# Differential attention on one core: the value products of a head written by block of keys instead of by block of queries

## The chip, the core and the metric

The kernel runs on one core of a Trainium2 chip. The core has TensorE (PE in the rows, with its weight loads as PEld), VectorE (DVE), ScalarE (ACT), GpSimd (POOL) and the queue that issues most transfers (SP). The metric is the device time of one execution in microseconds, lower is better, as the median of several runs.

## What is computed

The program is two transformer blocks over 512 tokens of width 1024. The change lies in the second block, in its differential attention with four heads; each head has two softmax maps over keys of 64 dimensions, and one value matrix of 128 columns:

```python
def diff_attention_causal(q, k, v, lam):
    ...
    def block(args):
        q_blk, i = args                                  # 128 queries
        s = jnp.einsum('bhmqd,bhmkd->bhmqk', q_blk, k).astype(jnp.float32) * scale
        s = jnp.where(kpos[None, :] <= qpos[:, None], s, -jnp.inf)
        p = jax.nn.softmax(s, axis=-1)
        a = p[:, :, 0] - lam * p[:, :, 1]
        return jnp.einsum('bhqk,bhkd->bhqd', a.astype(v.dtype), v)
...
        dq = rms_norm(dq, diff_q_gain[l])
        dk = rms_norm(dk, diff_k_gain[l])
        o_diff = diff_attention_causal(dq, dk, dv, lam)
        o_diff = rms_norm(o_diff, diff_subln[l]) * (1.0 - lam_init)
```

Beside it the block has a retention branch, whose products (rv, rq, rk, rg below) come next in the program, then the output product, cross attention and a feed-forward part.

## The kernel before

Every large product takes three passes of TensorE over split operands (a high and a low part of each, helper `mm3`, lines 199 to 201): `ws` makes one tile of 128 output columns for all 512 tokens with 8 x 3 products of 512 columns, `ts` one block of 128 tokens. Weights are loaded by SP into `wraw` (three buffers) and split by ACT (line 181) and DVE (line 182) into `whi` and `wlo`. The products write to a PSUM pool named `mm` with two banks; when a tile is complete, its evacuation function empties it. A second pool, `tp`, has two banks too, and a third, `at2`, has two pairs of banks.

The section of the change runs so: `ts` makes the values `dvn` of all four heads; then for heads 0 and 1, and after that for heads 2 and 3, `ws` makes the queries (two tiles, evacuated by `ev_dq`) and the keys (two tiles, `ev_dk`), and `diff_head(h)` is called for each of the two heads. The evacuation (`qk_norm`) copies the tile to `raw` on DVE, squares it on ACT, splits the squares (`sq`, `sqh`, `sql`), sums them on PE into a bank of `tp` (line 318), takes Ln and Exp on ACT (lines 310 and 311, tile `rb`), and multiplies on DVE (lines 1189 and 1196).

`diff_head(h)` takes a bank of `tp` for the transposed output `oT` of the head at its very beginning. For each of four blocks of 128 queries, i = 0 to 3, it makes the scores of both maps against the i + 1 blocks of keys that the mask leaves (line 1210, a pair of `at2`), subtracts the mask and finds the maxima on DVE, takes the exponentials on ACT (line 1217), combines the maps on DVE (lines 1219 and 1220), transposes each block of 128 x 128 on PE (line 1223), copies the transposed blocks to `aT` on ACT (line 1225), and multiplies each block of keys with the values into 128 columns of `oT` (line 1227). After the last block of queries `oT` is normed: squares and their split (`hsq`, `hsqh`, `hsql`), sums on PE into `at2`, Ln and Exp (`hrb`), the multiply on DVE (line 1231), which is the last that reads `oT`, and the split into `mxd`.

The order is not written by hand. A scheduler puts the instructions of each engine in a fixed order when the program is built; it pulls the products of the next stage (the queries and keys of heads 2 and 3 during heads 0 and 1, the retention values `rv` after that) into the gaps of the softmax. Each engine then works in that order, and waits at an instruction whose operands or buffers are not ready.

Of the kernel before, what the change touches and what calls it, by code (L numbers as in the profile page):

```python
# [8 lines left out]
F32 = mybir.dt.float32  # L9
# [11 lines left out]
S = 512  # L21
# [61 lines left out]
def body(tc, a, out):  # L83
    nc = tc.nc
    V, A, T, G = nc.vector, nc.scalar, nc.tensor, nc.gpsimd
    es = ExitStack()

    def pool(name, bufs, side=None, space=None, stack=None):
        kw = {}
        if side:  # L90
            kw["side"] = side
        if space is not None:
            kw["space"] = space
        return (stack or es).enter_context(tc.tile_pool(name=name, bufs=bufs, **kw))
# [21 lines left out]
    def psum(tag, name="ps"):  # L116
        if tag == "at":
            return banks[1][0].tile([128, 512], F32, name=name, tag="at", bufs=banks[1][1])
        return ps.tile([128, 512], F32, name=name, tag=tag, bufs=2)

    def psum2(tag="at2"):
        return banks[1][0].tile([128, 2, 512], F32, name=tag, tag=tag, bufs=banks[1][2])
# [141 lines left out]
    def hilo(hi, lo, src):  # L264
        A.copy(hi, src)  # L265
        last_lo[:] = [V.tensor_sub(lo, src, hi.bitcast(F32))]  # L266
# [40 lines left out]
    def rms_bcast(m, n, p, w=S, rbufs=2, name="rb"):  # L307

        q = p.tile([128, S], F32, name=name, bufs=rbufs)[:, :w]
        A.activation(q, m, AF.Ln, bias=epsc, scale=1.0 / n)  # L310
        A.activation(q, q, AF.Exp, scale=-0.5)
        return q
# [847 lines left out]
    tb = pool("tb", 1, side="right", stack=tst)  # L1160

    def tmp_(name, bufs):
        return tb.tile([128, S], F32, name=name, tag=name, bufs=bufs)
# [3 lines left out]
    def pair_(name, bufs):  # L1167
        return tb.tile([128, 2, S], F32, name=name, tag=name, bufs=bufs)

    w2 = a["w_in_2"][0]  # L1170
    dqn, dkn, dvn = {}, {}, {}

    def sq_sums(tag, ones, o, name):
        q = tmp_(name, 1)
        A.activation(q, o, AF.Square)
        hl = [tb.tile([128, S], F32R, name=name + n, bufs=2 if name == "sq" else 1) for n in "hl"]
        hilo(*hl, q)
        return sums(tag, ones, *hl)

    def qk_norm(o):  # L1180
        raw = tmp_("raw", 4)
        V.tensor_copy(raw, o)
        return raw, rms_bcast(sq_sums("tp", ones64r, o, "sq"), 64, tb)

    def ev_dq(c):
        def f(t, o):
            raw, rb = qk_norm(o)
            dqn[c + t] = slot2("dq")
            V.scalar_tensor_tensor(dqn[c + t], raw, gq8, rb, op0=OP.mult, op1=OP.mult)
        return f  # L1190

    def ev_dk(c):
        def f(t, o):
            raw, rb = qk_norm(o)
            dkn[c + t] = slot2("dk")
            V.scalar_tensor_tensor(dkn[c + t], raw, col("diff_k_gain_2"), rb, op0=OP.mult, op1=OP.mult)
        return f
# [4 lines left out]

    def diff_head(h):
        oT = psum("tp")
        for i in range(4):
            n = 128 * (i + 1)
            o = psum2()
            for m in range(2):
                ms = slice(64 * m, 64 * m + 64)
                T.matmul(o[:, m, :n], dqn[h][ms, i * 128:(i + 1) * 128], dkn[h][ms, :n], start=True, stop=True)  # L1210
            V.tensor_add(o[:, :, n - 128:n], o[:, :, n - 128:n], negdf[:, None, :].to_broadcast([128, 2, 128]))
            st = sp.tile([128, 2, 3], F32, name="dmx", bufs=4)
            V.reduce_max(st[:, :, 0], o[:, :, :n], axis=AX)
            V.tensor_scalar(st[:, :, 0], st[:, :, 0], -1.0, None, op0=OP.mult)
            pp = pair_("pp", 3)[:, :, :n]
            for m in range(2):
                A.activation(pp[:, m], o[:, m, :n], AF.Exp, bias=st[:, m, 0:1], accum_out=st[:, m, 1:2])
            V.reciprocal(st[:, :, 2], st[:, :, 1])
            V.tensor_scalar(pp[:, 1], pp[:, 1], st[:, 1, 2:3], lam, op0=OP.mult, op1=OP.mult)
            V.scalar_tensor_tensor(pp[:, 0], pp[:, 0], st[:, 0, 2:3], pp[:, 1], op0=OP.mult, op1=OP.subtract)  # L1220
            pt = o[:, 0, :n]
            for j in range(i + 1):
                T.transpose(pt[:, j * 128:(j + 1) * 128], pp[:, 0, j * 128:(j + 1) * 128], ident)  # L1223
            aT = tmp_("aT", 2)[:, :n]
            A.copy(aT, pt)
            for j in range(i + 1):
                T.matmul(oT[:, i * 128:(i + 1) * 128], dvn[j][:, h * 128:(h + 1) * 128], aT[:, j * 128:(j + 1) * 128],  # L1227
                         start=(j == 0), stop=(j == i))
        rb = rms_bcast(sq_sums("at2", onesr, oT, "hsq"), 128, tb, rbufs=1, name="hrb")
        y = tmp_("hsq", 1)  # L1230
        V.scalar_tensor_tensor(y, oT, gdf[:, h:h + 1], rb, op0=OP.mult, op1=OP.mult)
        for i in range(2):
            mx[i][4 + h] = mp.tile([128, S], F32R, name="mxd", tag="mxd", bufs=8)
        hilo(mx[0][4 + h], mx[1][4 + h], y)

    ts(w2, 8, 3072, 4, hT, ev_dv)
    for c in (0, 2):
        ws(w2, 8, 2048 + c * 128, 2, hT, S, ev_dq(c))
        ws(w2, 8, 2560 + c * 128, 2, hT, S, ev_dk(c))
        for h in (c, c + 1):  # L1240
            diff_head(h)
# [13 lines left out]
        A.copy(rg[t], o)  # L1255

    def rotated(o, scale):
        raw = tmp_("raw", 4)
        A.activation(raw, o, AF.Copy, scale=scale)
        sw = tmp_("sw", 2)  # L1260
        for g in range(4):
            src = g ^ 1
            nc.scalar.dma_start(sw[g * 32:(g + 1) * 32, :], raw[src * 32:(src + 1) * 32, :])
        V.tensor_mul(raw, raw, ct)
        V.tensor_mul(sw, sw, st_)
        return raw, sw

    def ev_rq(c):
        def f(t, o):
            raw, sw = rotated(o, 1.0)  # L1270
            rq[c + t] = slot2("rq")
            V.tensor_add(rq[c + t], raw, sw)
        return f

    def ev_rk(c):
        def f(t, o):
            raw, sw = rotated(o, 0.125)
            rk_[c + t] = slot2("rk")
            V.tensor_add(rk_[c + t], raw, sw)
        return f  # L1280
# [65 lines left out]
    oT = (xa.tile([128, 8, S], F32R, name="xoh"), xa.tile([128, 8, S], F32R, name="xol"))  # L1346
# [67 lines left out]
    aT = (fp.tile([128, NH, S], F32R, name="aTh"), fp.tile([128, NH, S], F32R, name="aTl"))  # L1414
# [58 lines left out]
```

## Time and profile before

| | |
|---|---|
| time, median of 3 runs | 1596.85 us (1596.2 to 1598.96) |
| time of the profiled execution | 1597.8 us |
| span of the profiled execution | 1596.0 us |
| PE busy | 1555.6 us, 97% of the span |
| DVE, ACT busy | 945.1 us (59%), 821.0 us (51%) |
| mean granted clock of PE | 0.996 |
| value products of the four heads (line 1227) | 80 records, first start 884.0 us, last 964.9 us |
| differential attention, first score to last value product | 876.4 to about 965 us |

Starts are counted from the beginning of the span. The page divides the span into 40 slices of about 40 us; the section of the change lies in the 22nd to 24th. A product of float32 operands is recorded as two records, so that the 40 value products stand as 80. A record of a product lasts beyond the start of the next one, since they are pipelined: what a product costs the engine is read from start to start, and its own duration says when its result is there.

### The profile page before, as it was taken

How to read it: one execution, taken by the hardware profiler on the slowest of the kernel's cores; microseconds unless marked ns; L12 is line 12 of the kernel's file. 1: busy time of each engine (PE TensorE's matmuls, PEld its weight loads, DVE VectorE, ACT ScalarE, POOL GpSimd, SP SyncE). 2: the span in 40 equal slices, each digit the busy share in tenths (PEclk: the TensorE clock that was granted, in tenths of full speed). 3: DMA queues.
4: the chain of work that ended last, by engine and by line, in shares of the span. 5: the costliest groups of instructions: out<-in, count | busy, mean ns of one | idle time of the engine just before them, and what ended most of it. 6: DMA issues, size and time to landing. Idle time of an engine off the chain costs nothing. (4 is left out here: it accounts for less than half of the span.)

```text
span 1596.0 us, 19930 instructions
## 1 busy us (share of the span) xinstructions
PE 1555.6 (97%) x7535; PEld 1208.0 (76%) x7535; DVE 945.1 (59%) x1379; ACT 821.0 (51%) x1279; POOL 69.8 (4%) x85
## 2 busy tenths in 40 slices
PE   7999999999999999999989999999999999999998
PEld 6887776678877777777677668668778888888887
DVE  6458937725647999998755865556655333333231
ACT  5445547753446888888765754434444332232120
POOL 3000000000011211110010000000000000000000
PEclk9999999999999999999999999999999999999999
DMA  7230231143679999999954114223212333333331
GB/s 224 80 106 1 68 91 40 53 134 104 211 245 327 347 368 360 362 355 374 362 185 139 54 52 121 73 91 115 79 54 72 100 93 95 103 93 96 103 119 40
DMA packets 203067, 242.85 MB, mean 152 GB/s; under 512 B 10400, under 2 KB 133560, under 8 KB 202968
## 3 DMA queue, kind: packets, MB, share of 16 engines
q1 hardware_dynamic: 188800, 205.43, 39.0%
q0 software_dynamic: 7056, 24.27, 5.4%
q10 hardware_dynamic: 7112, 11.85, 2.3%
q8 instruction: 60, 0.98, 0.3%
q14 instruction: 39, 0.32, 0.1%
HBM read 223.69 MB, written 15.73 MB: 150 GB/s over the span
## 5 line engine op out<-in xcount | busy, mean ns | idle before, releaser
L182 DVE TENSOR_TENSOR wlo<-wraw,whi 128x1024 fp32r<-128x1024 f32 x210 | 256.0, 1223 | 288.4 <-ACT whi L181 280.9
L181 ACT CAST whi<-wraw 128x1024 fp32r<-128x1024 f32 x210 | 220.5, 1051 | 394.9 <-PE ps L200 276.9
L199 PE MATMUL ps<-hTh,whi 128*128 128x512 f32 (+1 forms) x912 | 349.0, 383 | 1.3 <-DVE fsg L1423 0.8
L200 PE MATMUL ps<-hTl,whi 128*128 128x512 f32 (+1 forms) x912 | 348.6, 383 | 0.9 <-DVE hTl L266 0.9
L201 PE MATMUL ps<-hTh,wlo 128*128 128x512 f32 (+1 forms) x912 | 348.0, 382 | 0.0
L182 DVE TENSOR_TENSOR wlo<-rx,whi 128x1024 fp32r<-128x1024 f32 x176 | 210.5, 1220 | 38.2 <-ACT whi L181 37.0
L181 ACT CAST whi<-rx 128x1024 fp32r<-128x1024 f32 x176 | 182.7, 1049 | 51.8 <-PE ps L201 35.0
L199 PEld LDWEIGHTS ps<-hTh,whi 128*128 128x128 f32 x912 | 172.1, 189 | 38.7 <-issue 5.1
L200 PEld LDWEIGHTS ps<-hTl,whi 128*128 128x128 f32 x912 | 172.2, 189 | 34.7 <-issue 2.7
L201 PEld LDWEIGHTS ps<-hTh,wlo 128*128 128x128 f32 x912 | 172.0, 189 | 33.3 <-issue 2.0
L199 PE MATMUL ps<-whi,XT 128*96 128x512 f32 x256 | 102.2, 399 | 1.8 <-ACTq L1055 1.8
L201 PE MATMUL ps<-whi,XT 128*96 128x512 f32 x256 | 102.5, 400 | 0.0
L200 PE MATMUL ps<-wlo,XT 128*96 128x512 f32 x256 | 101.6, 397 | 0.1
L199 PE MATMUL ps<-whi,hTh 128*128 128x512 f32 x192 | 77.6, 404 | 0.2 <-ACT hTh L265 0.2
L201 PE MATMUL ps<-whi,hTl 128*128 128x512 f32 x192 | 77.1, 402 | 0.0
L200 PE MATMUL ps<-wlo,hTh 128*128 128x512 f32 x192 | 76.9, 401 | 0.0
L199 PE MATMUL ps<-whi,aTh 128*128 128x512 f32 x176 | 68.5, 389 | 0.0
L200 PE MATMUL ps<-wlo,aTh 128*128 128x512 f32 x176 | 68.5, 389 | 0.0
L201 PE MATMUL ps<-whi,aTl 128*128 128x512 f32 x176 | 68.5, 389 | 0.0
L1423 DVE TENSOR_TENSOR fsg<-fsg,ps 128x512 f32<-128x512 f32 x22 | 15.1, 687 | 76.4 <-PE ps L201 76.4
L199 PEld LDWEIGHTS ps<-whi,XT 128*96 128x96 f32 x256 | 41.7, 163 | 19.0 <-ACTq L1055 2.5
L200 PEld LDWEIGHTS ps<-wlo,XT 128*96 128x96 f32 x256 | 41.8, 163 | 18.0 <-DVE wlo L182 0.6
(453 smaller groups left out, 2505.1 us busy)
## 6 DMA issues: line engine op xcount, KB each, us to landing
wraw<-in_w_in_dram SPq DMA_DIRECT2D x72, 512.0 KB, 3.9
rx<-in_w_exp_gate_dram SPq DMA_DIRECT2D x58, 512.0 KB, 12.3
rx<-in_w_exp_down_dram SPq DMA_DIRECT2D x58, 512.0 KB, 12.4
rx<-in_w_exp_up_dram SPq DMA_DIRECT2D x52, 512.0 KB, 12.2
wraw<-in_w_gate_dram SPq DMA_DIRECT2D x22, 512.0 KB, 3.9
wraw<-in_w_up_dram SPq DMA_DIRECT2D x22, 512.0 KB, 3.9
wraw<-in_w_down_dram SPq DMA_DIRECT2D x22, 512.0 KB, 3.9
wraw<-in_w_out_dram SPq DMA_DIRECT2D x16, 512.0 KB, 3.8
```

The lines of the kernel that those rows point to most:

```text
L181: i1 = A.copy(hi, w)
L182: i2 = V.tensor_sub(lo, w, hi.bitcast(F32))
L199: T.matmul(o, lh, rh, start=first, stop=False)
L200: T.matmul(o, lh, rl, start=False, stop=False)
L201: T.matmul(o, ll, rh, start=False, stop=last)
L1423: V.tensor_mul(sg[t], sg[t], o)
```

## The change

The four blocks of queries of a head now leave their transposed probabilities in one tile `aTw` of 128 x 4 x 512 (block of keys, query), with one buffer, in place of `aT` of 128 x 512 with two. When all four are there, four value products are made, one for each block of keys j, over all the queries that see it: 512, 384, 256 and 128 columns, accumulated in `oT`. The multiplications of the mask's blocks are the same as before. To make room for the tile, the buffers of `raw` go from four to two, in the norm of queries and keys and in the rotation of the retention branch. Lines behind the tile's own move down by one.

```diff
     def qk_norm(o):
-        raw = tmp_("raw", 4)
+        raw = tmp_("raw", 2)
...
     def diff_head(h):
         oT = psum("tp")
+        aT = tb.tile([128, 4, S], F32, name="aTw", bufs=1)
         for i in range(4):
...
-            aT = tmp_("aT", 2)[:, :n]
-            A.copy(aT, pt)
-            for j in range(i + 1):
-                T.matmul(oT[:, i * 128:(i + 1) * 128], dvn[j][:, h * 128:(h + 1) * 128], aT[:, j * 128:(j + 1) * 128],
-                         start=(j == 0), stop=(j == i))
+            A.copy(aT[:, :i + 1, i * 128:(i + 1) * 128], pt.rearrange("p (j t) -> p j t", t=128))
+        for j in range(4):
+            T.matmul(oT[:, j * 128:], dvn[j][:, h * 128:(h + 1) * 128], aT[:, j, j * 128:],
+                     start=(j == 0), stop=(j == 3))
...
     def rotated(o, scale):
-        raw = tmp_("raw", 4)
+        raw = tmp_("raw", 2)
```

What the scheduler makes of it is seen on PE in head 1, the second of the first two. Before the change, PE sums the squares of the queries of head 2 (ps_8424) and of head 3 (ps_8471) between the blocks of queries of head 1, whose output is ps_8286; ps_8532 is the tile of the keys of head 3 that is being made:

```order
L318 MATMUL ps_8424<-sqh_8420,ones64r_203 128x512
L318 MATMUL ps_8424<-sql_8421,ones64r_203 128x512
L1223 MATMUL at2_8304<-ident_103,pp_8311 128x128 x2
L200 MATMUL ps_8532<-hTl_7704,whi_8528 128x512
L201 MATMUL ps_8532<-hTh_7703,wlo_8529 128x512
L199 MATMUL ps_8532<-hTh_7703,whi_8528 128x512
L1227 MATMUL ps_8286<-aT_8319,dv_7916 128x128
L1227 MATMUL ps_8286<-aT_8319,dv_7943 128x128
L1210 MATMUL at2_8344<-dk_8185,dq_8091 128x512 x2
L318 MATMUL ps_8471<-sqh_8467,ones64r_203 128x512
L318 MATMUL ps_8471<-sql_8468,ones64r_203 128x512
```

The sums stand between value products of the first blocks of queries, with main products around them. At the end of head 1, still before the change, products of the retention values (ps_8797) lie around the last transposes and the last value products:

```order
L1223 MATMUL at2_8344<-ident_103,pp_8351 128x128 x4
L201 MATMUL ps_8797<-whi_8781,hTl_7704 128x512
L318 MATMUL ps_8565<-sql_8562,ones64r_203 128x512
L199 MATMUL ps_8797<-whi_8787,hTh_7703 128x512
L200 MATMUL ps_8797<-wlo_8788,hTh_7703 128x512
L1227 MATMUL ps_8286<-aT_8361,dv_7916 128x128
L1227 MATMUL ps_8286<-aT_8361,dv_7943 128x128
L1227 MATMUL ps_8286<-aT_8361,dv_7970 128x128
L1227 MATMUL ps_8286<-aT_8361,dv_7997 128x128
```

Nothing there stands alone: two or three main products lie between the transposes and the value products that need them. After the change, from the last transposes of head 1 on, with ps_8277 as its output, ps_8406 and ps_8453 as the sums of the queries of heads 2 and 3, at2_8355 as the sums of the head's own norm, and ps_8761 as the first tile of the retention values:

```order
L1224 MATMUL at2_8327<-ident_103,pp_8334 128x128 x4
L1227 MATMUL ps_8277<-aTw_8278,dv_7916 128x512
L1227 MATMUL ps_8277<-aTw_8278,dv_7943 128x384
L1227 MATMUL ps_8277<-aTw_8278,dv_7970 128x256
L1227 MATMUL ps_8277<-aTw_8278,dv_7997 128x128
L318 MATMUL ps_8406<-sqh_8402,ones64r_203 128x512
L318 MATMUL ps_8406<-sql_8403,ones64r_203 128x512
L318 MATMUL ps_8453<-sqh_8449,ones64r_203 128x512
L318 MATMUL ps_8453<-sql_8450,ones64r_203 128x512
L318 MATMUL at2_8355<-hsqh_8351,onesr_239 128x512
L318 MATMUL at2_8355<-hsql_8352,onesr_239 128x512
L199 MATMUL ps_8761<-whi_8739,hTh_7703 128x512
```

The sums of the queries of heads 2 and 3 have moved from the middle of head 1 to behind its value products, and no main product is left between the last transposes and the first row of ps_8761. Ahead of these rows stand three transposes of the block before, and ahead of those 13 main products behind the head's last scores.

ACT shows the same place. Before, from the copy of the last weights in head 1 on (ps_8532 is the keys of head 3, aT_8361 the last transposed block, ps_8286 the head's output):

```order
L181 CAST whi_8793<-wraw_8791 128x1024
L1175 ACTIVATE sq_8559<-ps_8532 128x512
L265 CAST sqh_8561<-sq_8559 128x512
L1225 COPY aT_8361<-at2_8344 128x512
L310 ACTIVATE rb_8568<-ps_8565,epsc_98 128x512
L311 ACTIVATE rb_8568<-rb_8568 128x512
L1175 ACTIVATE hsq_8367<-ps_8286 128x512
L265 CAST hsqh_8369<-hsq_8367 128x512
L310 ACTIVATE hrb_8376<-at2_8373,epsc_98 128x512
L311 ACTIVATE hrb_8376<-hrb_8376 128x512
```

There the square of the key tile (sq_8559), which empties a bank of `mm`, stands ahead of the last copy. After, from the last copy on:

```order
L1225 COPY aTw_8278<-at2_8327 128x4x128
L1175 ACTIVATE hsq_8349<-ps_8277 128x512
L310 ACTIVATE rb_8409<-ps_8406,epsc_98 128x512
L265 CAST hsqh_8351<-hsq_8349 128x512
L311 ACTIVATE rb_8409<-rb_8409 128x512
L310 ACTIVATE rb_8456<-ps_8453,epsc_98 128x512
L310 ACTIVATE hrb_8358<-at2_8355,epsc_98 128x512
L311 ACTIVATE rb_8456<-rb_8456 128x512
L311 ACTIVATE hrb_8358<-hrb_8358 128x512
L1175 ACTIVATE sq_8494<-ps_8467 128x512
```

The square that empties a bank of `mm` (sq_8494, of ps_8467, the keys of head 2) has moved behind eight instructions that follow the head's value products. ps_8761, which takes the bank of ps_8467, waits for it on PE.

From the first scores of the retention branch on PE's order is the same as before; that of SP is the same throughout.

## Rows read from the trace of the kernel before

**Rows 1.** The page's busy time, share and instructions of PE and ACT.
```profile
PE 1555.6 (97%) x7535; PEld 1208.0 (76%) x7535; DVE 945.1 (59%) x1379; ACT 821.0 (51%) x1279; POOL 69.8 (4%) x85
```

**Rows 2.** Busy time by stretch (PE, PEld, DVE, ACT, POOL, granted clock, DMA): the section.
```profile
876.00:965.00 89.00, 87.58 (x431) 61.37 (x429) 63.94 (x130) 56.69 (x130) 0.00 (x0) 1.00 0.20 56
```

**Rows 3.** Waits of PE, 860 to 1080 us: us in total, times, longest.
```profile
PE at L1223 <- DVE pp L1220: 1.2, 3, 0.6
```

**Rows 4.** Timeline of PE in head 0: start, us, line, tile, shape, records.
```profile
884.02 0.49 PE L1227 MATMUL ps<-aT,dv 128*128 128x128 f32 x2
884.35 0.42 PE L1223 MATMUL at<-ident,pp 128*128 128x128 f32 x2
...
885.54 0.71 PE L1227 MATMUL ps<-aT,dv 128*128 128x128 f32 x4
886.18 1.13 PE L1210 MATMUL at<-dk,dq 64*128 64x512 f32 x4
...
892.37 0.94 PE L1227 MATMUL ps<-aT,dv 128*128 128x128 f32 x6
893.07 0.48 PE L201 MATMUL ps<-hTh,wlo 128*128 128x512 f32 x1
893.38 0.60 PE L1223 MATMUL at<-ident,pp 128*128 128x128 f32 x4
...
894.05 0.40 PE L200 MATMUL ps<-hTl,whi 128*128 128x512 f32 x1
894.28 0.40 PE L201 MATMUL ps<-hTh,wlo 128*128 128x512 f32 x1
...
894.75 1.06 PE L1227 MATMUL ps<-aT,dv 128*128 128x128 f32 x8
895.57 0.48 PE L200 MATMUL ps<-hTl,whi 128*128 128x512 f32 x1
```

**Rows 5.** Timeline of PE: float32 products of 256 columns in cross attention.
```profile
1143.04 1.46 PE L1376 MATMUL ps<-knT,xqn 128*128 128x256 f32 x6
1144.15 0.58 PE L201 MATMUL ps<-hTh,wlo 128*128 128x512 f32 x1
```

**Rows 6.** Timeline of PE in head 2: its last scores and its last transposes.
```profile
932.05 1.13 PE L1210 MATMUL at<-dk,dq 64*128 64x512 f32 x4
...
939.35 0.60 PE L1223 MATMUL at<-ident,pp 128*128 128x128 f32 x4
```

**Rows 7.** Timeline of ACT: the last copy of head 0.
```profile
894.02 0.59 ACT L1225 COPY aT<-at 128x512 f32<-128x512 f32 x1 [1.70 <-PE at L1223]
```

**Rows 8.** Timeline of ACT behind the last copy of head 1.
```profile
919.05 0.59 ACT L1225 COPY aT<-at 128x512 f32<-128x512 f32 x1 [1.67 <-PE at L1223]
919.53 0.69 ACT L310 ACTIVATE rb<-ps,epsc 128x512 f32<-128x512 f32 x1
920.26 0.63 ACT L311 ACTIVATE rb<-rb 128x512 f32<-128x512 f32 x1
920.89 0.60 ACT L1175 ACTIVATE hsq<-ps 128x512 f32<-128x512 f32 x1
```

**Rows 9.** Timeline of PE: the end of a wait in the first block's experts.
```profile
787.94 0.55 PE L1002 MATMUL ps<-ident,act 96*128 96x96 f32 x4 [2.62 <-DVE act L995]
```

**Rows 10.** Busy time by stretch of 1 us, as in rows 2: two idle stretches.
```profile
790.00:791.00 1.00, 1.00 (x4) 0.64 (x3) 0.00 (x0) 0.00 (x0) 0.00 (x0) 0.55 1.04 403
791.00:792.00 1.00, 1.00 (x4) 0.69 (x3) 0.00 (x0) 0.90 (x1) 0.00 (x0) 0.50 1.08 416
792.00:793.00 1.00, 1.00 (x4) 0.55 (x3) 0.82 (x1) 0.15 (x1) 0.00 (x0) 0.50 1.05 393
793.00:794.00 1.00, 1.00 (x5) 0.70 (x4) 0.40 (x1) 0.34 (x1) 0.00 (x0) 0.74 1.05 381
...
844.00:845.00 1.00, 0.00 (x0) 0.00 (x0) 0.25 (x1) 0.69 (x2) 0.00 (x0) 1.00 0.69 242
```

**Rows 11.** Waits of SP's queue, 860 to 1130 us: what the weight loads waited for.
```profile
SPq L179 <- DVE wlo L182: 223.7, 29, 32.0
```

## The prediction

> **What bounds the kernel now.** I read the busy shares first: PE 97%, ACT 51% [rows 1]. Then the section of the change by stretch: PE is busy 87.58 of 89 us from 876 to 965 us, at a granted clock of 1.00, while ACT works 56.69 us [rows 2]. Then the waits: for the softmax PE waits 1.2 us in all, three times, never above 0.6 us [rows 3]. So the section lasts as long as PE's own work, because the scheduler has main products to put wherever a head makes PE wait. Two questions decide: what PE's work shrinks by, and whether it still has something to do at every point of the new order.
>
> **The value products.** In head 0 the four bursts of value products take, from their start to the next start, 0.33, 0.64, 0.70 and 0.82 us, together 2.49 us [rows 4]; four heads 10.0 us. The product behind a burst runs 0.31 instead of 0.23 us [rows 4], for 16 bursts 1.3 us: 11.3 us in all.
>
> After the change a head has one burst of 8 records. What does a wide record cost? No value product of more than 128 columns is in the trace. The nearest row has the same kind of operands and 256 columns: 6 records last 1.46 us, and the next product starts after 1.11 us [rows 5]; five steps with a last record of some 0.38 us give 0.216 us a record. For 128 columns, 8 records last 1.06 us, seven steps and 0.27 us, so 0.113 us a record [rows 4]. Twice the columns cost 1.9 times as much. On that line 512, 384, 256 and 128 columns cost 0.43, 0.32, 0.216 and 0.113 us, twice each: 2.16 us a head, with 0.08 us for the product behind 2.24 us, and 9.0 us for four heads. The sum of columns is the same (1280) before and after; only starts of bursts are saved, 11.3 - 9.0 = 2.3 us. I take **-2.0 us**, a little less, since the first record of a burst waits for its weights and the copy. The near end is -1.0. The far end comes from the split products, where one record of 512 columns takes 0.23 us [rows 4]: were a wide float32 record as cheap, a head would cost about 1.4 us and the saving would be 5.8 us.
>
> The Trainium skill (TensorE: Matmul & The Clock Gate, section on the back-to-back issue gap) gives about 81 ns a product at 128 columns and 131 ns at 512 for streams of loads and products. By that, as an estimate, 80 records would cost 6.5 us and the 32 new ones about 3.4 us, a saving of 3.1 us in place of 2.0; the 0.113 us at 128 columns and 0.216 us at 256 speak against it here.
>
> **The copies.** 16 copies with the same elements, now with rows of 128 written apart. No such copy is in the trace; the last of a head takes 0.59 us [rows 7]. I cost the change at nothing. Were it a tenth slower, the one that lies on the path below would cost 0.06 us; the others lie beside PE's work, as ACT is busy for 64% of the section [rows 2].
>
> **What the move does to the order.** The first write of a head's output, which takes its bank of `tp`, moves from the first block of queries to the end of the head. The order printed above shows that in head 1 all sums for the queries of heads 2 and 3, which need a bank of `tp` as well, now stand behind that write. Without the sums there is no norm, without the norm `raw` isn't freed, and with two buffers of `raw` instead of four and two banks of `mm` nothing further can be produced: both banks hold finished key tiles. So behind the head's last scores PE has 13 main products and then none. The stall has three parts.
>
> (a) From the last scores to the last transposes. In head 0 that was 893.38 - 886.18 = 7.2 us [rows 4], in head 2 939.35 - 932.05 = 7.3 us [rows 6]. After the change PE has in it the scores, about 1.06 us (886.18 to the next start, and so in each head), 13 x 0.23 = 3.0 us of main products and about 0.3 us of transposes: 4.4 us. It idles 2.8 us by that. The scores of the third and fourth block now lie somewhat further apart, so that DVE and ACT have less queued up: 2.1 us as the low end. I take 2.5.
>
> (b) From the last transposes to the value products: 894.75 - 893.38 = 1.37 us in head 0 [rows 4], with the copy in it [rows 7]. PE's own share is some 0.36 us; where three main products lay, nothing lies now: 1.0 us.
>
> (c) From the value products to the first product of ps_8761. That waits for the bank of ps_8467, which ACT empties with the ninth instruction behind the value products (hsq, rb, hsqh, rb, rb, hrb, rb, hrb, sq). From start to start such instructions take (920.89 - 919.05) / 3 = 0.61 us, 0.48 at the least and 0.73 at the most [rows 8]: nine take 5.5 us, between 4.3 and 6.6. PE has six sums in it, 1.4 us at the 0.23 us of a main product. It idles 4.1 us, between 2.9 and 5.2. DVE's side of the same wait (normed queries, then the copy to `raw`) has fewer instructions and should not be last.
>
> Together 2.5 + 1.0 + 4.1 = **+7.6 us**, between 6.0 and 9.0; before, the same stretch idled about 0.2 us. Net +7.4. In the other three heads the waits for the softmax stay what they are, 1.2 us in three places [rows 3]; I count nothing for them, give or take 1 us. The smaller `raw` in the rotation costs nothing: each rotation also needs one of two `sw` buffers until the same addition, before as after, and PE's order there is unchanged.
>
> **The clock.** After 2.62 us of idle PE, followed by four small transposes and another short wait [rows 9], the granted clock fell to 0.50, the 1.2 GHz level, at about 790 us and was back at 1.00, 2.4 GHz, within 794 us. The four stretches of 1 us show 0.55, 0.50, 0.50 and 0.74: 1.7 us of full clock were lost [rows 10]. After an idle stretch of 1 us at 844 us it did not fall [rows 10]. The new stall has idle stretches of about 2.5 and 2.5 us with little between: it is more like the first. I take one such fall, **+1.7 us**; none is the low end, two the high one (3.4 us, of which some lies under the wait for ACT).
>
> **Sum.** -2.0 + 7.4 + 1.7 = +7.1 us. The profiled execution took 1597.8 us, so 1604.9 us for one like it. The median of the runs lies 0.95 us lower, at 1596.85: the forecast is **1604.0 us**, 0.45% slower.
>
> **Rivals.**
>
> *The clock doesn't fall.* The pieces of work inside the stall keep it up, as at 844 us [rows 10]. Then 1596.85 - 2.0 + 7.4 = 1602.3 us.
>
> *A longer stall or a second fall.* ACT at the slow end of part (c) adds 1.1 us, and a fall that starts inside the stall slows the value products on its path as well, up to another 1.7 us: about 1606.5 us.
>
> *Wide records are cheap.* If a float32 record of 512 columns cost about the 0.23 us of a split one, the saving would be 5.8 us and the time 1596.85 - 5.8 + 7.4 + 1.7 = 1600.2 us, and without a fall of the clock 1598.5. The 256 columns at 0.216 us [rows 5] speak against it.
>
> *The stall is given back: not slower.* The weight loads could run ahead during the stall, and a later stage that waits for them would start with its weights at hand. In the output product eight loads of 512 KB follow close on each other; were they to start at the same time as before, that stage would absorb the whole delay, and -2.0 us would remain: 1594.9 us. It decides at what the loads wait for. SP's queue waits 223.7 us, in 29 waits, for the DVE split that frees `wraw` [rows 11], and that split waits for `whi`, which PE's products free. So the loads move with PE, and I give this little.
>
> **How the numbers follow.** The forecast has 0.50, no fall of the clock 0.22, the longer stall 0.14, cheap wide records 0.08, the stall given back 0.04; 0.02 is left. The measurement of this kernel tells about 0.2% (3.2 us) from no change, so the line lies at 1600.05 us. Slower: forecast, no fall, longer stall and a part of the rest, 0.88. Same: most of the cheap records, 0.08. Faster: 0.04. The range is 1600.0 to 1607.5 us: below, the low ends of the stall without a fall of the clock (-2.0 + 5.8 = +3.8, 1600.7) and a little of the cheap records; above, the slow end of ACT with two falls (-1.0 + 8.5 + 3.4 = +10.9, 1607.7).
>
> **What would show it.** In the profile after, the value products stand as 32 records, the 512-column ones at about 0.43 us from start to start; at 0.23 the third rival holds. At the end of head 1 PE idles about 2.5 us ahead of its last transposes, 1 us ahead of the value products, and some 4 us, in pieces between the sums, ahead of the first product of the retention values, which the square of the key tile on ACT (line 1175) releases. The granted clock shows 0.5 for some 3.4 us within about 10 us of that, or stays at 1.00. The first scores of the retention branch start 5 to 7 us later than before, and that distance stays to the end; a distance that shrinks in the output product would speak for the fourth rival. If the waits at the end of head 1 add up to less than 4 us, parts (a) and (c) are wrong.

## The result and the profile after

The changed kernel takes 1606.94 us (median, 1604.77 to 1609.79), the kernel before beside it 1596.25 us (1594.13 to 1598.96): 10.7 us or 0.67% slower, ratio 1.0067 with a 95% interval of 1.0053 to 1.0081. The profiled execution of the changed kernel took 1609.79 us, with a span of 1608.0 us; its granted clock was 0.991 on average, before 0.996. Among the executions behind the medians below, one each of three kernels was far slower (1634.85, 1918.58 and 5318.6 us); the medians hold them, which moves those by 0.13 us at most, and the ratios leave them out.

On the page PE is as busy as before, by share; its busy time is 6.6 us longer [rows 1], although it executes 48 records less:

```profile
PE 1562.2 (97%) x7487; PEld 1208.5 (75%) x7487; DVE 946.1 (59%) x1379; ACT 821.0 (51%) x1279; POOL 69.9 (4%) x85
```

**Where the time went.** From the first scores of differential attention to the first scores of the retention branch PE executes the same products in both kernels, except for the value products: 384 main products, 64 records of scores, 40 of transposes, 18 of sums. That makes this section a good yardstick. It ran from 876.43 to 1001.27 us before, 124.8 us, and from 876.90 to 1012.02 us after, 135.1 us: the loss of 10.3 us lies in it. The span grew by 12.0 us. Of the other 1.7 us, 0.5 us lie ahead of the section and 1.2 us behind it; in a second trace of the same kernel (below) it was 0.4 us behind it.

The groups of instructions of that section show what PE waited for. The columns are line, operation, shapes and count, busy time and mean ns of one, and behind the second bar the idle time just before them with its releasers. First two groups of the kernel before, then five of the changed one:

```profile
L1227 PE MATMUL ps<-aT,dv 128*128 128x128 f32 x80 | 12.4, 286 | 0.0
L1223 PE MATMUL at<-ident,pp 128*128 128x128 f32 x40 | 7.3, 281 | 1.3 <-DVE pp L1220 1.2
```

```profile
L199 PE MATMUL ps<-whi,hTh 128*128 128x512 f32 x32 | 13.5, 421 | 2.3 <-ACT sq L1175 2.3
...
L1227 PE MATMUL ps<-aTw,dv 128*128 128x512 f32 (+3 forms) x32 | 11.1, 498 | 0.7 <-ACT aTw L1225 0.7
L1224 PE MATMUL at<-ident,pp 128*128 128x128 f32 x40 | 7.5, 285 | 3.5 <-DVE pp L1221 2.9 <-DVE dmx L1215 0.5
L318 PE MATMUL ps<-sqh,ones64r 128*128 128x512 f32 x5 | 2.3, 456 | 0.9 <-ACT rb L310 0.9
...
L318 PE MATMUL at<-hsql,onesr 128*128 128x512 f32 x4 | 1.9, 478 | 0.2 <-DVE hsql L266 0.2
```

The idle time in these groups grew from 1.3 to 7.6 us. The timeline of PE shows that nearly all of the growth is one place, the end of head 1 (start, duration, line, tile, shape, records, and in brackets the wait ahead of it):

```profile
908.67 1.13 PE L1211 MATMUL at<-dk,dq 64*128 64x512 f32 x4
...
912.81 0.50 PE L1224 MATMUL at<-ident,pp 128*128 128x128 f32 x3
915.34 0.63 PE L1224 MATMUL at<-ident,pp 128*128 128x128 f32 x4 [2.02 <-DVE pp L1221]
916.64 4.11 PE L1227 MATMUL ps<-aTw,dv 128*128 128x512 f32 x8 [0.67 <-ACT aTw L1225]
920.50 0.48 PE L318 MATMUL ps<-sqh,ones64r 128*128 128x512 f32 x1
920.82 0.40 PE L318 MATMUL ps<-sql,ones64r 128*128 128x512 f32 x1
922.07 0.51 PE L318 MATMUL ps<-sqh,ones64r 128*128 128x512 f32 x1 [0.86 <-ACT rb L310]
922.42 0.39 PE L318 MATMUL ps<-sql,ones64r 128*128 128x512 f32 x1
922.64 0.44 PE L318 MATMUL at<-hsqh,onesr 128*128 128x512 f32 x1
923.31 0.50 PE L318 MATMUL at<-hsql,onesr 128*128 128x512 f32 x1 [0.23 <-DVE hsql L266]
926.11 0.50 PE L199 MATMUL ps<-whi,hTh 128*128 128x512 f32 x1 [2.30 <-ACT sq L1175]
```

Between the last scores and the last transposes stand the 13 main products and then nothing; behind the transposes nothing; behind the value products only sums, held once by ACT and once by DVE, until the first main product, which waits 2.30 us for ACT. The five waits add up to 6.08 us. Compare [rows 4], where main products lie on both sides of each burst of value products.

One row here is longer than it should be: this burst of value products takes 3.86 us to the next start, while head 0's takes 2.08 us:

```profile
895.47 2.33 PE L1227 MATMUL ps<-aTw,dv 128*128 128x512 f32 x8
897.55 0.48 PE L201 MATMUL ps<-hTh,wlo 128*128 128x512 f32 x1
```

The stretches of 1 us say why. The columns are as in [rows 2]; the number to read is the granted clock, third from the right:

```profile
916.00:917.00 1.00, 0.36 (x1) 0.30 (x2) 0.32 (x1) 0.59 (x1) 0.00 (x0) 1.00 0.08 16
917.00:918.00 1.00, 1.00 (x2) 0.33 (x1) 0.00 (x0) 0.00 (x0) 0.00 (x0) 0.55 0.23 69
918.00:919.00 1.00, 1.00 (x3) 0.61 (x2) 0.00 (x0) 0.00 (x0) 0.00 (x0) 0.50 0.97 291
919.00:920.00 1.00, 1.00 (x3) 0.60 (x3) 0.00 (x0) 0.00 (x0) 0.00 (x0) 0.50 0.51 152
920.00:921.00 1.00, 1.00 (x5) 0.68 (x4) 0.00 (x0) 0.15 (x1) 0.00 (x0) 0.74 0.04 12
...
927.00:928.00 1.00, 1.00 (x5) 0.80 (x4) 1.00 (x3) 0.50 (x2) 0.00 (x0) 0.67 0.00 0
928.00:929.00 1.00, 1.00 (x4) 0.81 (x3) 0.29 (x1) 0.32 (x1) 0.00 (x0) 0.50 0.00 0
929.00:930.00 1.00, 1.00 (x4) 0.71 (x4) 0.00 (x0) 0.66 (x2) 0.00 (x0) 0.50 0.00 0
930.00:931.00 1.00, 1.00 (x4) 0.81 (x3) 0.43 (x1) 1.00 (x3) 0.00 (x0) 0.62 0.00 0
```

The clock fell to 0.50, the 1.2 GHz level, twice: within the stretch from 917 us, after the waits of 2.02 and 0.67 us, and within that from 927 us, after those of 0.86, 0.23 and 2.30 us. Each fall took 1.71 us of full clock. Before, it stood at 1.00 in the whole section, most of which [rows 2] shows.

**The account of the section.** In the timeline each row of PE can be charged with the time from its start to the next start, less the wait named at the next row. Summed by kind (us):

| | before | after | difference |
|---|---|---|---|
| waits | 1.23 | 7.47 | +6.24 |
| value products | 9.81 | 10.10 | +0.29 |
| 384 main products | 92.98 | 94.98 | +2.00 |
| scores, transposes, sums | 20.82 | 22.57 | +1.75 |
| sum | 124.84 | 135.12 | +10.28 |

The first fall of the clock is in the value products (3.86 - 2.08 = 1.78 us) and the second in the main products and sums (1.71 us). Without them the value products went from 9.81 to 8.32 us. So the account reads: value products -1.49, waits +6.24, clock +3.49, and +2.04 us that remain. About half of that lies in products with a wait behind them: the three sums ahead of a wait hold PE for 0.40 to 0.50 us each, and the main products ahead of four shorter waits of the section for 0.39 to 0.50 us, where the next product would start after 0.2 to 0.3 us if it were there. The rest is spread over steps whose neighbours changed: eleven main products stand directly ahead of scores instead of three, for instance, and take 0.33 us to the next start there, against 0.24 us ahead of another main product.

### The profile page after: what moved, and what is told of

Read it like the earlier page. It is cut to its first block, busy times and chain, and to the rows that moved or that the text cites. A ratio compares the mean times of both kernels' runs of the same rounds, so it can differ in the third digit from the quotient of the medians.

```text
span 1608.0 us, 19845 instructions
## 1 busy us (share of the span) xinstructions
PE 1562.2 (97%) x7487; PEld 1208.5 (75%) x7487; DVE 946.1 (59%) x1379; ACT 821.0 (51%) x1279; POOL 69.9 (4%) x85
```

## Experiments

Theory 1: the stall comes from the place of the output's first write. With wide products the first value product needs all four blocks of queries; the bank of `tp` is taken then, and the sums for heads 2 and 3 queue behind it. Theory 2: the two buffers of `raw`, or the one buffer of `aTw`, are what stalls. A further question is whether the falls of the clock belong to the stall. All runs are told with the median, the ratio to the kernel before on the same chip with its interval, and the length of the section of the account, from the first scores of differential attention to the first scores of retention, in the trace. In three traces of the changed kernel, or of it with an edit that leaves every engine's order as it is, that length was 135.1, 135.0 and 135.1 us, and in two of the kernel before, likewise, 124.8 and 124.9 us, so it tells tenths of a microsecond where the whole time does not.

### The output's bank taken early, products narrow

```diff
-        for j in range(4):
-            T.matmul(oT[:, j * 128:], dvn[j][:, h * 128:(h + 1) * 128], aT[:, j, j * 128:], ...)
+            for j in range(i + 1):
+                T.matmul(oT[:, i * 128:(i + 1) * 128], ..., aT[:, j, i * 128:(i + 1) * 128], ...)
```

> The changed kernel with one part undone: the value products stand block of queries by block of queries again (40 products of 128 columns), so the head's output takes its bank of tp at the first block; the one wide probability tile and the two raw buffers stay. Theory 1 (the stall comes from the place of the output's first write, which holds the sums behind it): the three waits at the end of head 1 are gone (below 1 us in all), the granted clock stays at 1.00 from 905 to 935 us, first retention scores within 1 us of the kernel before (about 1001 to 1003 us), 1595 to 1598 us. Theory 2 (two raw buffers and a single probability tile are what stalls): waits of 6 us or more stay, 1604 to 1608 us.

Measured: 1598.0 us, ratio 1.0016 (1.0007 to 1.0025); section 126.1 us. The granted clock is 1.00 through the section, and the five waits at the end of head 1 are gone. That is at the upper edge of what theory 1 expected and far from theory 2: 9.0 of the 10.3 us are gone, although this run gives up the saving of the wide products as well. The 1.3 us that it keeps are left to the buffers.

### The output's bank taken early, products wide

```diff
             A.copy(aT[:, :i + 1, i * 128:(i + 1) * 128], ...)
+            if i == 0:
+                T.matmul(oT[:, :128], dvn[0][...], aT[:, 0, :128], start=True, stop=True)
         for j in range(4):
-            T.matmul(oT[:, j * 128:], dvn[j][...], aT[:, j, j * 128:], ...)
+            c = max(j, 1) * 128
+            T.matmul(oT[:, c:], dvn[j][...], aT[:, j, c:], ...)
```

> The changed kernel, but the product of block 0 with itself (128 columns) is made right behind the first copy, so that the output takes its bank of tp at the head's start; the other columns stand at the head's end in wide products of 384, 384, 256 and 128 columns. Theory 1: no stall at the end of head 1, no fall of the clock there, and what wide products save in starts is left over: 1593.5 to 1597 us, 0.5 to 2.5 us below the run with narrow products. Theory 2 (buffers): 1603 to 1608 us. If wide products at the head's end stall PE by themselves, whatever the bank, the waits at the end of head 1 stay at 6 us and the time above 1603 us.

Measured: 1594.96 us, ratio 1.0000 (0.9991 to 1.0009); section 124.4 us. One product of 128 columns, written at the head's start, undoes the loss, with the tile, its single buffer and two `raw` buffers in place. The timeline of PE at the end of head 1, without its main products, shows the mechanism:

```profile
904.78 0.48 PE L318 MATMUL ps<-sqh,ones64r 128*128 128x512 f32 x1
905.10 0.39 PE L318 MATMUL ps<-sql,ones64r 128*128 128x512 f32 x1
905.66 1.13 PE L1211 MATMUL at<-dk,dq 64*128 64x512 f32 x4
906.72 0.50 PE L318 MATMUL ps<-sqh,ones64r 128*128 128x512 f32 x1
...
915.24 0.60 PE L1224 MATMUL at<-ident,pp 128*128 128x128 f32 x4
...
916.60 2.12 PE L1230 MATMUL ps<-aTw,dv 128*128 128x384 f32 x8
```

The sums of the next tiles (line 318) lie ahead of the head's wide products, at 904.8 and 906.7 us, and not behind them as in the changed kernel (920.5 us). PE has main products to the end, and its longest wait in the section is 1.0 us. Against the run with narrow products the section is 1.7 us shorter, and the time 3.0 us, a little more than the 0.5 to 2.5 us expected. Against the changed kernel the section is 10.7 us shorter: that is what the late first write costs with the products wide in both, but for the one of 128 columns.

### Another bank for the output

```diff
-        oT = psum("tp")
...
+        oT = psum2()[:, 0]
         for j in range(4):
             T.matmul(oT[:, j * 128:], ...)
```

> The changed kernel with all value products wide and at the head's end, but the output takes a bank of the at2 pairs instead of tp, so that the sums need not stand behind it. Theory 1: the order of tp alone is the cause, so the waits ahead of the last transposes and the first product of ps_8761 at the end of head 1 go, 1594 to 1598 us. Theory 2 (buffers): 1603 to 1608 us. A third outcome: the scores of the next head, which need the pairs too, wait for the output's bank; then the waits stand at the scores of each head and the time is 1598 to 1603 us.

Measured: 1597.54 us, ratio 1.0016 (1.0007 to 1.0024); section 126.7 us; the clock stays at 1.00. All value products are wide and at the head's end, as in the changed kernel, and the stall is gone. So it is not the late products themselves that stall PE but what queues behind their bank. Its largest wait in the section is 1.5 us, for the split of a head's squares:

```profile
969.67 0.50 PE L318 MATMUL at<-hsql,onesr 128*128 128x512 f32 x1 [1.46 <-DVE hsql L266]
```

### Four raw buffers again

```diff
-        raw = tmp_("raw", 2)
+        raw = tmp_("raw", 4)
-            pp = pair_("pp", 3)[:, :, :n]
+            pp = pair_("pp", 2)[:, :, :n]
```

(both at each of their two places)

> The changed kernel with four raw buffers again; to make room, the softmax tile pp has two buffers instead of three, which leaves the order of the kernel before as it is. Theory 1: the sums still stand behind the output's first write, but some 21 more main products come ahead of or into the stall, so the waits at the end of head 1 come down from about 9 us to 3 to 6 us, with no fall or one fall of the clock: 1598.5 to 1603 us. Theory 2 (two raw buffers are the cause): the stall is gone, 1593.5 to 1597 us.

> The changed kernel with four raw buffers and two of pp, as in the run before it under the same description, for a second trace: there the median was 1606.4 us while the traced execution took 1603.57 and showed one fall of the clock at the end of head 1. If the falls come and go from execution to execution, the second trace shows the same waits and none or two falls there, and lies nearer its median. If the same single fall stands again, the executions differ elsewhere. Median 1604 to 1607 us by the first run; by the waits alone, which came down by about 3 us against the change, 1601 to 1604 us.

Measured: 1606.4 us, ratio 1.0069 (1.0055 to 1.0083), and in the second run 1601.69 us, ratio 1.0051 (1.0036 to 1.0065); section 130.9 us in both traces. The first median missed what either theory expected, the second lies within theory 1. The traces agree with each other and with theory 1: the sums still stand behind the value products, but 32 main products instead of 13 lie between the last scores and the value products, and the waits of the section come to 3.6 us instead of 7.5. At the end of head 1 they are 2.5 us, below the 3 to 6 us expected. The timeline of the second:

```profile
914.45 2.34 PE L1227 MATMUL ps<-aTw,dv 128*128 128x512 f32 x8
916.54 0.48 PE L318 MATMUL ps<-sqh,ones64r 128*128 128x512 f32 x1
...
920.23 0.50 PE L318 MATMUL ps<-sqh,ones64r 128*128 128x512 f32 x1 [0.39 <-ACT sqh L265]
920.96 0.50 PE L318 MATMUL ps<-sql,ones64r 128*128 128x512 f32 x1 [0.23 <-DVE sql L266]
922.92 0.53 PE L199 MATMUL ps<-whi,hTh 128*128 128x512 f32 x1 [1.47 <-ACT sq L1175]
```

The stall ahead of the value products is gone, and they take 2.09 us at a clock of 1.00; the stall behind them remains, and so does the fall behind that, one of 1.7 us in both traces. What the two medians differ by, 4.7 us for one kernel, isn't in the section, which is alike in both traces. The first scores started at 874.9 us in the first trace and at 872.4 us in the second, so 2.5 us were lost ahead of it, 2.0 us of them in one place of the expert stage: the same products start 0.3 us later at 820 us and 2.3 us later at 826 us. The granted clock, third from the right, was down there in the first trace and up in the second:

```profile
819.50:826.50 7.00, 6.37 (x19) 5.14 (x20) 5.67 (x7) 4.74 (x11) 0.53 (x1) 0.51 0.89 265
819.50:826.50 7.00, 6.52 (x34) 4.97 (x35) 5.33 (x7) 5.20 (x10) 0.54 (x1) 1.00 0.93 272
```

The executions without a trace go the same way: over the twelve of this kernel the mean granted clock runs from 0.990 to 0.995 and the time from 1608.75 to 1600.81 us, about 1 us for each microsecond of full clock lost. Why the clock falls in one execution and not in another stays open.

### The changed kernel again, and with two pp buffers

The first of the two runs is the changed kernel without an edit. In the second only `pp` has two buffers instead of three.

> The changed kernel, not edited, beside the others on one chip, for a second trace of it: the run with four raw buffers came out as slow as the change (1606.4 us) although its trace shows a shorter stall, so one trace of each does not settle what the stall costs in a usual execution. If the loss is the stall alone, the waits at the end of head 1 are those of the first trace (2.0, 0.7, 0.9, 2.3 us). If the falls of the granted clock to 0.5 are a fixed part of it, there are again two at the end of head 1, 1.7 us each; if they come and go, none or one, and the time lies 1.7 or 3.4 us below 1608. Expected: 1604 to 1608 us.

> The changed kernel with two pp buffers and two raw buffers, in the same order on every engine as the change: the control for the run with four raw buffers. Theory: as the change, 1605 to 1607.5 us, the same four waits at the end of head 1 and two falls of the clock. Rival: two pp buffers cost 2 us or more: 1608 us or above, and then four raw buffers did bring their 3 us.

Measured: 1605.8 us, ratio 1.0064 (1.0051 to 1.0077), section 135.0 us; and 1606.82 us, ratio 1.0071 (1.0058 to 1.0083), section 135.1 us. Both traces show the same waits at the end of head 1 as the first one (2.0, 0.7, 0.9, 2.3 us) and two falls of the clock, 1.7 us each, at the same two places. So in the three traced executions these falls do not come and go. The mean granted clock of all executions agrees: on these two chips the change lost 11.2 and 10.4 us of full clock on average, the kernel before 7.0 and 7.3 us (one execution of it, at 0.945 with an ordinary time, left out), and two falls are 3.4 us. Where the clock fell in an execution without a trace isn't shown. Two `pp` buffers cost nothing here. On the chip where they stood side by side, four `raw` buffers brought 1606.82 - 1601.69 = 5.1 us, against 4.2 us in the section.

### Two raw buffers alone, two pp buffers alone

```diff
-        raw = tmp_("raw", 4)
+        raw = tmp_("raw", 2)
```

in the kernel before, and in another run `pp` with two buffers instead of three there.

> The kernel before with two raw buffers instead of four, and nothing else. Theory 1 (two buffers cost nothing while the sums are not held up): within 1.5 us of the kernel before, 1594 to 1597 us. Rival: two buffers cost some 2.5 us by themselves, which would explain why the runs with narrow products and with the other bank, which have two as well, lie 2.3 to 2.8 us above the kernel before: 1597 to 1599 us.

> The kernel before with two pp buffers instead of three, in the same order on every engine: what the room for four raw buffers was bought with in the runs above. Theory: nothing, 1594 to 1596.5 us. Rival: exp of a block then waits for the transposes two blocks back, and it costs 2 us or more: 1597 to 1600 us, which would explain why the run with four raw buffers was not faster than the change and the early bank with four raw buffers not faster than with two.

Measured: with two `raw` buffers 1596.26 us, ratio 1.0008 (0.9999 to 1.0017), section 126.1 us; with two `pp` buffers 1596.03 us, ratio 1.0008 (0.9997 to 1.0018), section 124.9 us. The smaller `raw` costs 1.3 us in the section and less than this measurement tells in the whole. That is as much as the run with early narrow products lost there (126.1 us): beside it the wide tile with its one buffer costs nothing in the section. The trace with two `pp` buffers has one fall of the clock at 1081 us that no other trace shows, and none in the section.

### Early bank, wide products, four raw buffers

The run with the bank taken early, with the edit of `raw` and `pp` above.

> The run whose first value product takes the bank of tp at the head's start and whose others are wide at its end, now with four raw buffers again (and two of pp to make room). If two raw buffers cost some 2.5 us by themselves: 1591.5 to 1593.5 us, which would beat both kernels. If they cost nothing: 1594 to 1596 us, as with two.

Measured: 1597.12 us, ratio 1.0008 (0.9999 to 1.0017); section 125.2 us. The expectation failed by 1 us or more: four buffers bring nothing once the sums aren't held. No version was measurably faster than the kernel before.

### Added work in the stall

```diff
             A.copy(aT[:, :i + 1, i * 128:(i + 1) * 128], ...)
+            if h == 1 and i == 2:
+                for _ in range(2):
+                    T.matmul(oT[:, :384], dvn[0][...], aT[:, 0, :384], start=True, stop=True)
```

> The changed kernel with added work and nothing taken away: in head 1, behind the third block's copy, two products of 384 columns are made into the head's own output bank (1.3 us of PE at full clock; the value products write over them). They lie in the idle stretch ahead of the last transposes, and one pair of the sums for a later head moves ahead of the value products by it. If idleness ahead of the value products is what brings the clock down, the granted clock stays at 1.00 through head 1's value products, which take 2.1 us instead of 3.9, and in spite of more work the time falls by 1.7 us or more: 1602 to 1605 us. If the fall has another cause, the value products still take 3.9 us and the time is that of the change or up to 1 us above: 1606 to 1608.5 us.

Measured: 1599.32 us, ratio 1.0030 (1.0019 to 1.0040); section 129.1 us. With 1.4 us more to do PE is 6.5 us faster than with the change on the same chip. The timeline of PE:

```profile
908.70 1.56 PE L1228 MATMUL ps<-aTw,dv 128*128 128x384 f32 x4 [0.72 <-ACT aTw L1225]
910.10 0.60 PE L1224 MATMUL at<-ident,pp 128*128 128x128 f32 x4
910.45 0.48 PE L318 MATMUL ps<-sqh,ones64r 128*128 128x512 f32 x1
910.77 0.40 PE L318 MATMUL ps<-sql,ones64r 128*128 128x512 f32 x1
911.37 2.42 PE L1230 MATMUL ps<-aTw,dv 128*128 128x512 f32 x8 [0.21 <-ACT aTw L1225]
913.55 0.48 PE L318 MATMUL ps<-sqh,ones64r 128*128 128x512 f32 x1
913.87 0.40 PE L318 MATMUL ps<-sql,ones64r 128*128 128x512 f32 x1
915.57 0.50 PE L318 MATMUL at<-hsqh,onesr 128*128 128x512 f32 x1 [1.30 <-ACT hsqh L265]
916.29 0.49 PE L318 MATMUL at<-hsql,onesr 128*128 128x512 f32 x1 [0.23 <-DVE hsql L266]
916.63 0.46 PE L199 MATMUL ps<-whi,hTh 128*128 128x512 f32 x1
```

The added products take the place of the wait of 2.0 us, of which 0.72 us remain ahead of them, and the value products take 2.18 us instead of 3.86: the clock is 1.00 in the whole section. Over its executions, the one of 1634.85 us left out, the loss of full clock is 7.0 us on average, as in the kernel before. The time came out below what was expected, since two things went that the expectation had not counted on together: with one pair of sums ahead of the value products the time from the value products' start to the first main product is 5.26 us instead of 9.47, and without its long wait the second fall is gone too. That the first fall hangs on the idle time ahead of it is what this run shows, and both the added products and the moved sums shorten that idle time; how much of the rest is the clock's and how much the moved sums', this run cannot part.

## Why the prediction was right, and where it was off

- **The mechanism** was as forecast: the sums for heads 2 and 3 behind the output's first write, `raw` and `mm` full, 13 main products and then none. The experiments on the bank show it. Their sections, taken one after the other, part the 10.3 us: two `raw` buffers +1.3 us (124.8 to 126.1), the wide tile with narrow products nothing (126.1), wide products with the bank taken early -1.7 us (124.4), and the late first write +10.7 us (135.1).
- **Value products**, forecast 2.16 us a head and 0.08 us for the product behind: measured 2.08 us in heads 0, 2 and 3. The line through [rows 4] and [rows 5] held, and the rival of cheap wide records fell. (The -2.0 us held some 1 us for the products behind the bursts, which the account has among the main products; the bursts alone were forecast at -1.3 and measured at -1.49. That 1 us did not come: it was counted for 16 bursts, but before the change only eight of them have a main product behind them, and the main products without the second fall became 0.3 us longer, not shorter.) The Trainium skill (TensorE: Matmul & The Clock Gate, back-to-back issue gap) gives 81 ns a product of 128 columns and 131 ns one of 512 in a stream; by that, as an estimate, the saving would have been the 3.1 us of the prediction. The trace disagrees: the eight records of a burst, of 128 to 512 columns, took 0.26 us each on average.
- **Part (a)**, forecast 7.2 to 7.3 us from the last scores to the last transposes with 2.5 us idle: 6.67 us with 2.02 idle. **Part (b)**, 1.37 us with 1.0 idle: 1.30 us with 0.67 idle. **Part (c)**, 5.5 us from the value products to the first product of ps_8761: 926.11 - 920.50 = 5.61 us. Its length was right, and it ended where forecast, at the square of the key tile on ACT, the ninth instruction behind the value products:

```profile
920.85 0.60 ACT L1175 ACTIVATE hsq<-ps 128x512 f32<-128x512 f32 x1 [4.26 <-PE ps L1227]
...
925.47 0.58 ACT L1175 ACTIVATE sq<-ps 128x512 f32<-128x512 f32 x1
```

- PE was idle for 3.39 of those 5.61 us, not 4.1: the six sums took 2.2 us, where 6 x 0.23 = 1.4 us were forecast. A product with a wait behind it isn't overlapped by the next; it holds PE for its own length, 0.40 to 0.50 us. So the waits of the section grew by 6.2 us instead of 7.4, and 2.0 us came back, about half of them as longer steps ahead of waits. Both together are 8.3 us: 0.9 us above the forecast.
- **The clock** is the term that was mis-sized: forecast one fall, 1.7 us, with two as the high end; there were two, 3.5 us, in all three traces. The forecast compared the stall with the one wait of [rows 9] and didn't ask of each of its parts whether it was long enough for a fall of its own. It also let part of a second fall lie under the wait for ACT; in fact the first fall lay on the value products, on the path, and the second on main products with PE busy, so both count in full. Its other comparison, an idle stretch of 1 us at 844 us without a fall, was in fact a wait of 1.66 us:

```profile
845.65 1.29 PE L299 MATMUL ps<-ident,hn 128*128 128x128 f32 x8 [1.66 <-DVE hn L284]
```

- **The sum**: forecast -2.0 + 7.4 + 1.7 = +7.1 us; measured -1.5 + 8.3 + 3.5 = +10.3 us in the section. The time, 1606.94 us, is that of the rival with a second fall (1606.5 us), which had the smaller chance; it lies inside the range, and the direction was right. But only half of that rival came: there were two falls, while ACT was not at its slow end (part (c) took 5.61 us, not 6.6). Longer steps made up for that, so the agreement with 1606.5 us is in part luck. The upper end of the range was also summed with 8.5 us of net waits, where 9.0 - 0.2 = 8.8 belongs; it would have been about 1608 us.
- **Not given back.** The distance to the kernel before was 10.75 us at the first retention scores (1001.27 and 1012.02 us) and 12.0 us at the end, so the fourth rival fell. **The copies** needed no term: 0.59 us for the last of a head, as before [rows 7].
- **The smaller raw** was forecast to cost nothing in the rotation, and for the norm it was counted inside the stall alone. By itself it costs 1.3 us in the section, which the prediction did not have. From the first retention scores to the first scores of cross attention, three traces of the change took 122.5 to 123.6 us and the kernel before 122.5 us: nothing that can be told for the rotation.

## What to carry over

When operations are gathered at the end of a loop, ask which buffer they write first and who takes the next one of that pool: here a bank requested first but written last held up work of a later stage, and writing one small part of it early took the loss away. A stall on an engine at full load is to be costed with its parts, the products beside them at their full length, and each longer wait inside it as a possible fall of the clock of its own. To compare two orders, take the time between two places in the trace with the same work between them: it repeated to 0.1 us where the whole time varied by several.

## What the runs showed of the hardware

- **Falls of the clock repeated at one place of a fixed order, and not at another.** At the end of head 1 there were two in each of three traces of the change, one in both with four `raw` buffers, none in the one with the added work, and none in any of those without the stall. In the expert stage ahead of it, from 785 to 829 us, the loss of full clock varied from one trace to the next, in steps of 1.7 us: 6.8 and 5.1 us in two traces of the changed kernel, 5.1 and 3.4 us in two of that with four `raw` buffers, in the same order.
- **Short waits can do it together.** With four `raw` buffers the fall at 923 us came after waits of 0.17, 0.23, 0.39, 0.23 and 1.47 us with one to three sums between them; with the added work, waits of 0.72, 0.21, 1.30 and 0.23 us with more products between them brought none. Neither did a single wait of 1.46 us (another bank, 969.67 us) or of 1.66 us (kernel before, 845.65 us).
- **A float32 product costs by its columns.** 512, 384, 256 and 128 columns in two records each took 2.08 us from start to next start, in head 0 about 0.43, 0.32, 0.22 and 0.11 us a record, save the last, behind which the next product starts after 0.03 us; ten products of 128 columns, the same 1280 columns, 2.49 us in four bursts [rows 4].
